# Feed-forward input units: one 512-column product for high and low activations, against two 256-column ones

## The chip, the cores and the metric

The program runs on one core of a Trainium2 chip. The metric is the device time of one execution in microseconds (us). Matrix products run on TensorE (PE; its weight loads are listed as PEld), element-wise work on VectorE (DVE), ScalarE (ACT) and GpSimd (POOL), and SyncE (SP) issues nearly all transfers.

## What is computed

Two transformer blocks of two layers each, in float32, on 256 tokens of width 1024. The first block has, in each layer, a gated feed-forward half, a mixer of three branches, a cross-attention and a second feed-forward half, each followed by a layer norm; the second block has adaptive modulation, attention over a latent and a context stream, and one feed-forward half per layer. The part that matters here is the gated feed-forward:

```python
def swiglu_ffn(x, w_in, w_out):          # x (256, 1024), w_in (1024, 5632), w_out (2816, 1024)
    a, b = jnp.split(x @ w_in, 2, axis=-1)
    return (jax.nn.silu(a) * b) @ w_out
```

It is computed six times: four times in the first block and once in the first layer of the second block for two streams, and once in the last layer for one stream.

## The kernel before

**Precision by splitting.** A float32 operand x is kept as a high part h (x rounded to fp32r by an ACT copy, line 200) and a low part l = x - h (a DVE subtraction, line 201). A product is then three matmuls into the same PSUM bank: high weights times high activations, high weights times low activations, low weights times high activations (`mm3`, lines 203 to 207). Each matmul instruction loads its own stationary 128x128 block of weights.

**Units.** `ffn_in` (from line 356) computes the 5632 columns of `x @ w_in` in 22 units of 2x128 columns: 128 for the gate a, 128 for the value b. The first two units go through `groupB` (activations stationary, then a transpose); the other 20, j = 2 to 21, keep the weights stationary and stream the 256 tokens. For one stream, `colsA` (line 209) makes 8 steps k of `mm3` for c = 0 (a) into columns 0 to 255 of one bank of the pool `pj`, then 8 for c = 1 (b) into columns 256 to 511: 48 matmuls of 256 columns. ACT then reads a through Silu (line 396), and DVE multiplies it with b (line 397). Five of the six passes are of this kind, 100 units in all; the pass over two streams has its own branch (lines 384 to 390), in which the two streams of 256 tokens stand side by side in a `Joint`, and matmuls have 512 columns.

**Weights.** `weight` (line 162) loads a unit as two halves of 512 KB (here c = 0 and c = 1), each into one of 3 buffers `wf`; ACT makes `wh` (6 buffers), DVE makes `wl` (5 buffers). The SP queue issues the loads in order. Between them stand the loads of `wa` (one buffer), rows of the modulation weights of the second block, which DVE multiplies with the condition vectors (line 913, two products for each load). These products have nothing to do with the feed-forward; `mods` (line 929) spreads them over the units of the first block.

**Order.** The instructions go through a scheduler, which orders each engine's queue by priority and by its own model of the engines; an engine then runs its queue strictly in that order. `issue_after` ties a few instructions behind others.

**Activations.** `Split` (line 41) holds h and l of all 8 steps in four tiles, each of 4 steps of one kind. It is written by `put`, in the tail of a layer norm (line 282) or of a modulation (line 958): for each of two token blocks, two groups of four transposes into PSUM, each followed by one split of 128x512.

**After the units.** `ffn_out` (line 400) multiplies with `w_out` in 11 units of 24 matmuls of 512 columns, into four banks of the pool `pa`. Both pools have four banks.

## Time and profile before

| | |
|---|---|
| median of 3 runs | 2544.79 us (2539.27, 2544.79, 2544.91) |
| the profiled execution | 2539.28 us, span of its records 2537.5 us |
| PE busy | 2441.2 us of the span |
| DVE, ACT, POOL busy | 1654.8, 1176.4, 67.2 us |
| mean granted TensorE clock | 0.984 of full speed |
| moved by DMA | 425.74 MB |

The profile lists busy times by engine and by group of instructions, the chain of work that ended last, and for every idle time of an engine what ended it. A matmul's record is longer than the step from one matmul to the next, since they are pipelined: the pace is read from the starts in the timeline. In each of the single-stream passes the 20 units run from about 22 to 137, 566 to 682, 765 to 881, 1302 to 1418 and 2356 to 2471 us; the pass over two streams from about 1781 to 1999 us.

### The profile page before, as it was taken

To read this page: it belongs to the slowest core of one execution; us is meant where nothing else is said; L and a number is where in the kernel's file an instruction comes from. 1 tells how busy PE (TensorE), PEld (TensorE's weight loads), DVE (VectorE), ACT (ScalarE), POOL (GpSimd) and SP (SyncE) were. 2 spreads that over 40 slices of the span, in tenths; PEclk is the share of its full clock that TensorE was granted. 3 is DMA by queue.
4 is the path that set the end of the run, shared out by engine and by line. 5 is a ranking of instruction groups with operands and counts; after the bars stand their busy time and mean duration, and the time that the engine had idled before them with its cause. 6 is when DMAs were issued, how large, how long until landed. Compare 5 with 4: busy or idle time off the path is not lost.

```text
span 2537.5 us, 39368 instructions
## 1 busy us (share of the span) xinstructions
PE 2441.2 (96%) x15166; PEld 2138.2 (84%) x15166; DVE 1654.8 (65%) x3277; ACT 1176.4 (46%) x1948; POOL 67.2 (3%) x88
## 2 busy tenths in 40 slices
PE   8999999989999999999899999899999999998999
PEld 8987999869979979999789877677888887776997
DVE  6576766578677667766677776776554537655554
ACT  5445564444444444555544545654222324545542
POOL 0000100000000000100000000000000000131000
PEclk9999999999999999999999999999999999998999
DMA  7774535547757755446557642013456633433564
GB/s 266 225 252 160 167 116 186 182 141 253 236 174 250 234 189 179 143 147 210 173 174 234 227 157 81 24 42 111 157 189 192 215 98 107 122 56 126 183 191 141
DMA packets 139420, 425.74 MB, mean 168 GB/s; under 512 B 29192, under 2 KB 36064, under 8 KB 139104
## 3 DMA queue, kind: packets, MB, share of 16 engines
q1 hardware_dynamic: 139232, 423.22, 52.3%
q8 instruction: 119, 1.95, 0.3%
q14 instruction: 69, 0.57, 0.1%
HBM read 417.89 MB, written 5.28 MB: 167 GB/s over the span
## 4 chain that ended last, share of the span: by engine, by line
PE 82%; DVE 9%; DMA 3%; ACT 3%; issue 1%; POOL 0%; SPq 0%; ACTq 0%; POOLq 0%; DVEq 0%
PE pj L205 18%; PE pj L206 18%; PE pj L207 18%; PE pa L206 7%; PE pa L205 7%; PE pa L207 7%; PE pa L278 3%; DVE wl L201 2%; DMA k<-in_rpbF_dram 1%; ACT wh L200 1%; DMA wf<-in_mix_A_dram 1%; DVE mx L463 1%; DVE rq L261 1%; DVE k L201 1%; DVE k L315 1%
## 5 line engine op out<-in xcount | busy, mean ns | idle before, releaser
L200 ACT CAST wh<-wf 128x1024 fp32r<-128x1024 f32 (+2 forms) x652 | 672.8, 1034 | 924.3 <-PE pj L206 240.9
L201 DVE TENSOR_TENSOR wl<-wf,wh 128x1024 fp32r<-128x1024 f32 (+2 forms) x652 | 782.3, 1204 | 443.4 <-PE pj L207 129.8
L205 PE MATMUL pj<-k,wh 128*128 128x256 f32 (+1 forms) x2896 | 840.7, 290 | 0.0
L206 PE MATMUL pj<-k,wh 128*128 128x256 f32 (+1 forms) x2896 | 837.9, 289 | 0.0
L207 PE MATMUL pj<-k,wl 128*128 128x256 f32 (+1 forms) x2896 | 837.2, 289 | 0.0
L205 PEld LDWEIGHTS pj<-k,wh 128*128 128x128 f32 x2896 | 554.4, 191 | 13.9 <-issue 6.4
L206 PEld LDWEIGHTS pj<-k,wh 128*128 128x128 f32 x2896 | 553.9, 191 | 9.3 <-issue 2.0
L207 PEld LDWEIGHTS pj<-k,wl 128*128 128x128 f32 x2896 | 553.9, 191 | 6.8
L206 PE MATMUL pa<-wl,k 128*128 128x512 f32 x688 | 273.8, 398 | 0.8 <-DVE wl L201 0.8
L205 PE MATMUL pa<-wh,k 128*128 128x512 f32 x688 | 272.1, 396 | 2.4 <-ACT k L200 2.4
L205 PE MATMUL pj<-wh,k 128*128 128x512 f32 (+1 forms) x616 | 252.3, 412 | 11.8 <-ACT wh L200 6.5
L206 PE MATMUL pj<-wl,k 128*128 128x512 f32 (+1 forms) x616 | 251.1, 408 | 3.1 <-DVE wl L201 3.0
L913 DVE SCALAR_TENSOR_TENSOR k<-wa,cond 128x1024 bf16<-128x1024 f32 x160 | 193.6, 1222 | 70.4 <-DMA wa<-in_mod_wT_dram 69.8
L207 PE MATMUL pa<-wh,a 128*128 128x512 f32 x560 | 217.6, 389 | 0.0
L207 PE MATMUL pj<-wh,k 128*128 128x512 f32 (+1 forms) x496 | 201.1, 407 | 1.1 <-DVE k L201 1.0
L205 PEld LDWEIGHTS pa<-wh,k 128*128 128x128 f32 x688 | 128.8, 187 | 36.6 <-ACT k L200 3.5
L205 PEld LDWEIGHTS pj<-wh,k 128*128 128x128 f32 x616 | 120.7, 196 | 40.2 <-ACT k L200 8.2
L206 PEld LDWEIGHTS pa<-wl,k 128*128 128x128 f32 x688 | 129.2, 188 | 28.8 <-DVE wl L201 1.1
L206 PEld LDWEIGHTS pj<-wl,k 128*128 128x128 f32 x616 | 120.8, 196 | 29.6 <-DVE wl L201 5.6
L278 PE MATMUL pa<-ident,k 128*128 128x128 f32 x516 | 86.8, 300 | 48.4 <-DVE k L315 21.0
L278 PEld LDWEIGHTS pa<-ident,k 128*128 128x128 f32 x516 | 63.8, 152 | 76.6 <-DVE k L315 27.5
L207 PEld LDWEIGHTS pa<-wh,a 128*128 128x128 f32 x560 | 105.3, 188 | 25.0
(253 smaller groups left out, 2418.3 us busy)
## 6 DMA issues: line engine op xcount, KB each, us to landing
wf<-in_ffn_w_inA_dram SPq DMA_DIRECT2D x262, 512.0 KB, 4.4
wf<-in_ffn_w_outB_dram SPq DMA_DIRECT2D x132, 512.0 KB, 4.4
wf<-in_mix_A_dram SPq DMA_DIRECT2D x108, 512.0 KB, 3.7
wa<-in_mod_wT_dram SPq DMA_DIRECT2D x96, 512.0 KB, 4.3
wf<-in_w_branchA_dram SPq DMA_DIRECT2D x32, 384.0 KB, 3.2
wf<-in_od_w_dram SPq DMA_DIRECT2D x24, 512.0 KB, 4.9
wf<-in_w_mix_outB_dram SPq DMA_DIRECT2D x16, 512.0 KB, 4.4
wf<-in_w_outB_dram SPq DMA_DIRECT2D x16, 512.0 KB, 4.1
```

What stands on the lines that cost most here:

```text
L200: self.nc.scalar.copy(h, x)
L201: self.nc.vector.tensor_tensor(l, x, h.bitcast(F32), ALU.subtract)
L205: mm(ps, sh, mh, start=start, stop=False)
L206: mm(ps, sh, ml, start=False, stop=False)
L207: self.mark = mm(ps, sl, mh, start=False, stop=stop).ins
L261: V.scalar_tensor_tensor(y2, a, 3 * s * s, y, ALU.subtract, ALU.mult)
L278: self.nc.tensor.transpose(ps[:, i * P:(i + 1) * P], b, self.ident)
L315: z = V.scalar_tensor_tensor(y[:, s], y[:, s], rs, gb[1][:, s], ALU.mult, ALU.add)
L463: V.reduce_max(mx[:, i:i + 1], ps[:, a:b], axis=AX.X, negate=scale == 1.0)
L913: V.scalar_tensor_tensor(junk, w, 1.0, self.cond[:, s], ALU.mult, ALU.mult, accum_out=mod[:, n, s:s + 1])
```

## The change

The activations of the single-stream passes are laid out in a new class `Sides`: a tile holds, for two steps k, the high parts and then the low parts, so that h and l of a step are read as one operand of 2x256 columns. A new `colsD` uses it: for each k, high weights times (h, l) in one 512-column matmul, which leaves high-by-high in the first half of a bank and high-by-low in the second; then low weights times h, 256 columns, added in the first half. A unit takes two banks, one of `pj` for a and one of `pa` for b. To read a bank out, ACT copies its second half to a buffer `k1`, and DVE adds the first half. Silu then reads the buffer on ACT, and the product of gate and value is made on POOL. Layer norms and modulations write `Sides`, with two splits of 128x256 in place of one of 128x512.

```diff
+class Sides:
+    def __init__(self, net):
+        self.hl = [net.k4(F32R).rearrange("p (s k t) -> p s k t", s=2, k=2) for _ in range(KT // 2)]
+    def h(self, k, c=slice(None)):
+        return self.hl[k // 2][:, 0, k % 2, c]
+    def l(self, k, c=slice(None)):
+        return self.hl[k // 2][:, 1, k % 2, c]
+    def both(self, k):
+        return self.hl[k // 2][:, :, k % 2]
+    def put(self, net, i, c, y):
+        for j in range(2):
+            t = self.hl[2 * i + j]
+            net.split(t[:, 0, :, c], t[:, 1, :, c], y[:, 2 * j:2 * j + 2])
...
+    def colsD(self, ps, w, base, xs):
+        mm = self.nc.tensor.matmul
+        for k in range(KT):
+            wh, wl = w.at(base + k * P, P)
+            mm(ps.rearrange("p (s t) -> p s t", s=2), wh, xs.both(k), start=k == 0, stop=False)
+            self.mark = mm(ps[:, :T], wl, xs.h(k), start=False, stop=k == KT - 1).ins
...
     def load_split(self, src):
-        xs = Split(self, KT)
+        xs = Sides(self)
...
-            self.split(xs.hs[i], xs.ls[i], f)
+            xs.put(self, i, slice(None), f)
...
     def post_ln(self, acc, x, scale, l, i, eps, want_xs=True):
-        xs = Split(self, KT) if want_xs else None
+        xs = Sides(self) if want_xs else None
...
-                ps = self.pj()
+                ab = []
                 for c in range(2):
-                    self.colsA(ps[:, c * T:(c + 1) * T], w, c * KT * P, P, streams[0])
-                a = self.k1()
-                nc.scalar.activation(a, ps[:, :T], AF.Silu)
-                nc.vector.tensor_tensor(gs[j // 4][:, j % 4], a, ps[:, T:], ALU.mult)
+                    ps = self.ps() if c else self.pj()
+                    self.colsD(ps, w, c * KT * P, streams[0])
+                    ab.append(self.k1())
+                    nc.scalar.copy(ab[c], ps[:, T:])
+                    nc.vector.tensor_tensor(ab[c], ab[c], ps[:, :T], ALU.add)
+                nc.scalar.activation(ab[0], ab[0], AF.Silu)
+                nc.gpsimd.tensor_tensor(gs[j // 4][:, j % 4], ab[0], ab[1], ALU.mult)
...
     def first_block(self, dbg=None, depth=DEPTH):
-        xs = Split(self, KT)
+        xs = Sides(self)
...
-                self.split(xs.hs[i][:, c], xs.ls[i][:, c], f[i][:, c])
+                for j in range(k // 2, (k + n) // 2):
+                    self.split(xs.hl[j][:, 0], xs.hl[j][:, 1], f[i][:, 2 * j % 4:2 * j % 4 + 2])
...
     def modulating(self, x, mod, kind, s, xs=None, aside=False):
-        xs = xs or Split(self, KT)
+        xs = xs or Sides(self)
```

## Rows read from the trace of the kernel before

**Rows 1.** The page: busy time by engine, and the chain's shares.

```profile
PE 2441.2 (96%) x15166; PEld 2138.2 (84%) x15166; DVE 1654.8 (65%) x3277; ACT 1176.4 (46%) x1948; POOL 67.2 (3%) x88
...
PE 82%; DVE 9%; DMA 3%; ACT 3%; issue 1%; POOL 0%; SPq 0%; ACTq 0%; POOLq 0%; DVEq 0%
```

**Rows 2.** Busy us, first pass: PE, PEld, DVE, ACT, POOL; clock, DMA share, GB/s.

```profile
22.00:137.50 115.50, 115.50 (x964) 115.41 (x962) 71.97 (x86) 51.51 (x65) 0.00 (x0) 1.00 0.75 237
```

**Rows 3.** Timeline of PE, last pass (start, duration, line): 256-column matmuls.

```profile
2400.11 0.28 PE L205 MATMUL pj<-k,wh 128*128 128x256 f32 x1
2400.23 0.28 PE L206 MATMUL pj<-k,wh 128*128 128x256 f32 x1
```

**Rows 4.** Five units of the last pass: DVE busy on low weights `wl`; clock, DMA.

```profile
2384.80:2413.60 28.80, 12.24 (x10) 1.00 0.60 185
```

**Rows 5.** DVE's group on low weights, last pass, 2362 to 2471 us.

```profile
L201 DVE TENSOR_TENSOR wl<-wf,wh 128x1024 fp32r<-128x1024 f32 x38 | 46.5, 1224 | 44.6 <-PE pj L207 34.2 <-issue 10.4
```

**Rows 6.** The same for three times five units of the third pass.

```profile
765.30:794.10 28.80, 11.01 (x9) 1.00 0.81 258
794.10:822.90 28.80, 10.82 (x9) 1.00 0.72 237
822.90:851.70 28.80, 13.16 (x11) 1.00 0.74 236
```

**Rows 7.** DVE's groups, third pass, 771 to 845 us: busy, mean ns, idle before.

```profile
L201 DVE TENSOR_TENSOR wl<-wf,wh 128x1024 fp32r<-128x1024 f32 x24 | 29.1, 1221 | 3.8 <-ACT wh L200 3.6
L913 DVE SCALAR_TENSOR_TENSOR k<-wa,cond 128x1024 bf16<-128x1024 f32 x21 | 25.1, 1222 | 6.2 <-DMA wa<-in_mod_wT_dram 6.1
L397 DVE TENSOR_TENSOR k<-k,pj 128x256 f32<-128x256 f32 x12 | 5.0, 419 | 3.9 <-ACT k L396 3.9
```

**Rows 8.** Timeline of PE, two-stream pass: first and last of six 512-column matmuls.

```profile
1799.95 0.39 PE L206 MATMUL pa<-k,wh 128*128 128x512 f32 x1
...
1801.08 0.39 PE L205 MATMUL pa<-k,wh 128*128 128x512 f32 x1
```

**Rows 9.** Timeline of PE: a 256-column matmul ahead of a 512-column one, and the reverse.

```profile
880.50 0.28 PE L207 MATMUL pj<-k,wl 128*128 128x256 f32 x1
880.62 0.40 PE L205 MATMUL pa<-wh,k 128*128 128x512 f32 x1
...
2355.80 0.39 PE L207 MATMUL pj<-wh,k 128*128 128x512 f32 x1
2356.03 0.28 PE L206 MATMUL pj<-k,wh 128*128 128x256 f32 x1
```

**Rows 10.** Timeline of PE, last `ffn_out`: its widest step between 512-column matmuls.

```profile
2489.81 0.40 PE L206 MATMUL pa<-wl,k 128*128 128x512 f32 x1
2490.05 0.39 PE L207 MATMUL pa<-wh,a 128*128 128x512 f32 x1
```

**Rows 11.** Line 396: count, min/median/max ns.

```profile
L396 ACT ACTIVATE k<-pj x100: 363/377/387, 28.3 to 2471.6; 128x256 f32<-128x256 f32 x100
```

**Rows 12.** Groups with shapes apart: a 256-column PSUM copy, splits of either size.

```profile
L376 ACT COPY k<-pa 128x256 f32<-128x256 f32 x14 | 5.2, 374 | 3.8 <-PE pa L278 3.8
...
L200 ACT CAST k<-pa 128x512 fp32r<-128x512 f32 x30 | 17.5, 585 | 20.8 <-PE pa L278 18.5 <-PE pa L819 1.5
...
L200 ACT CAST k<-pa 128x256 fp32r<-128x256 f32 x24 | 9.1, 393 | 1.1 <-PE pa L1396 1.1
...
L201 DVE TENSOR_TENSOR k<-pa,k 128x512 fp32r<-128x512 f32 x30 | 20.0, 688 | 8.6 <-ACT k L200 8.2
...
L201 DVE TENSOR_TENSOR k<-pa,k 128x256 fp32r<-128x256 f32 x24 | 9.9, 420 | 16.1 <-ACT k L200 15.9
```

**Rows 13.** Timeline of the mixer, second layer: POOL products beside a weight split.

```profile
1013.03 1.55 DVE L201 TENSOR_TENSOR wl<-wf,wh 128x1024 fp32r<-128x1024 f32 x1 [0.54 <-PE pj L207]
...
1012.77 0.73 POOL L657 TENSOR_TENSOR a<-k,sc 128x256 f32<-128x256 f32 x1
1013.46 1.44 POOL L658 TENSOR_TENSOR a<-k,sc 128x128 f32<-128x128 f32 x1
```

## Prediction

> **What bounds the kernel now.** I read the page first, then the stretches of the passes the change touches, then the queues that feed them. The page says that PE is busy for 96% of the span and carries 82% of the chain that ended last [rows 1]. By stretches it is plainer still: in the first pass PE is busy for all of 115.50 us at full granted clock, beside 71.97 us of DVE, 51.51 of ACT and none of POOL [rows 2]. PE's own pace is read from the starts: matmuls of 256 columns follow each other every 120 ns [rows 3], so a unit of 48 costs 5.76 us, and a half of its weights (24 matmuls) lasts 2.88 us. A pass of 20 units takes 115.2 us, nearly what the stretch shows: in the five single-stream passes nothing but PE sets the end today.
>
> Close behind PE is what feeds it: the load, the ACT cast and the DVE subtraction of each half of weights. Five units use ten halves, which are 12.24 us of DVE's subtraction [rows 4]. In the last pass exactly that is made, and DVE idles mainly until PE gives a buffer back [rows 5]: feeding is faster than eating, and the five `wl` buffers are full. The third pass differs. In its first two stretches DVE makes only 11.01 and 10.82 us of it, and catches up in the third with 13.16 [rows 6]. There the modulation products stand in DVE's queue; between 771 and 845 us, 21 of them take 25.1 us, and the idle of 6.2 us ahead of them ends when their own load lands [rows 7]. PE lives on the reserve for some nine units. The second and fourth passes show the same pattern in the same view; one stands for the three. In the first, `mods` is called only from j = 10 on. So the question is twofold: what PE saves, and whether the feeding follows.
>
> **PE's saving.** Per step k, three 256-column matmuls become one of 512 and one of 256; the columns stay the same. Three cost 3 x 120 = 360 ns. The 512-column form with the same read pattern (two runs of 256) exists in the pass over two streams, and steps there by 226 ns: 1.13 us for the five steps from the first to the last row of [rows 8]. Does the mixture add up? A 256-column matmul ahead of a 512-column one took 120 ns, a 512 ahead of a 256 took 230 as rounded [rows 9]. I expect 347 ns, 13 less. The 512-column steps of `ffn_out`, whose operands have other roles, are up to 240 ns wide [rows 10]; that would leave nothing. I take 227, what the rounding leaves at most, by the pass whose operands have the same roles and layout. For 16 steps and 100 units [rows 11] that is 16 x 100 x 0.013 = 20.8 us, or 4.16 us for each pass; a unit falls to 5.55 us, a half to 2.78.
>
> The Trainium skill, page "TensorE: Matmul & The Clock Gate", section "Back-to-back issue gap", gives a matmul a fixed part of 2.5 ns beside its columns at the warm clock. By that the change would save 2.5 ns per step, 4 us in all. The rows show 120 ns where 256 columns at 2.4 GHz are 106.7, so a fixed part near 13 ns, and I go by them.
>
> **Readout.** Removed per unit: a Silu from PSUM (0.377 us, ACT [rows 11]) and a product on DVE (0.419 [rows 7]). Added: two ACT copies of 256 columns (0.374 each [rows 12]), two DVE adds of the form of the old product (0.42 each), a Silu from SBUF (not in the trace; 0.36 to 0.39 by the PSUM form), and a POOL product. ACT gains 0.75 us a unit, DVE 0.42. ACT is busy for 51.51 of 115.50 us in the first pass [rows 2], so its part is hidden by idle time. The waits are new: the adds wait for ACT, and Silu on ACT for a DVE add, with the weight casts queued behind it; POOL waits for both, with nothing behind it. Banks: a unit takes one of four in each pool, as deep as the four single banks today, and `ffn_out` reaches the bank of the last unit only after 15 matmuls of at least 0.226 us, 3.4 us after its start; I cost that at nothing, up to 0.5 us a pass if the last add is late.
>
> **The POOL product** is the least certain. One of 128x256 takes 0.73 us undisturbed. But beside it a weight subtraction, which reads two SBUF tiles, took 1.55 us, and the POOL operation after it 1.44 [rows 13], against 1.221 for such a subtraction alone [rows 7]: POOL and DVE shut each other out. So a unit can cost DVE up to 0.42 + 0.73 = 1.15 us. How much delays the feeding? Nothing, where it falls into DVE's idle time; that is 6.2 + 3.8 + 3.9 = 13.9 us over 12 units [rows 7], 1.16 a unit, but part of it is the wait for ACT, which will not shrink. I take 0.5 us a unit, near the idle ahead of the modulation products (6.2 / 12), with 0 and 1.15 as ends.
>
> The Trainium skill, "GPSIMD Engine Reference", section "1. Specifications", says that POOL shares its SBUF interface with VectorE and that instructions with two SBUF inputs contend. This case's row agrees (1.55 us against 1.22), and by that rule the third rival below would hold.
>
> **Feeding, pass by pass.** In the first two stretches of the third pass (11.01 + 10.82) / 1.221 = 17.9 halves are made in 57.6 us, 6.44 us a unit for nine units. Against 5.55 us the reserve shrinks by 9 x 0.89 = 8.0 us. Full, it is four halves (the fifth buffer back comes free as its own half ends) less one subtraction and its hand-over, 4 x 2.78 - 1.3 = 9.8 us: 1.8 are left, and every further 0.1 us a unit takes 0.9. With 0.5 us PE waits 4.5 - 1.8 = 2.7 us, so such a pass keeps 4.16 - 2.7 = 1.5. At 0 it keeps all; at 1.15 it loses 4.4. Three passes give 4.4 us (ends: 12.5 gained, 13 lost). The last pass has no modulation products and its reserve is full: 4.16. The first has them in its second half alone, but starts with little reserve: 3.5 (1.5 to 4.2).
>
> **Splits.** A put now makes two casts of 0.393 in place of one of 0.585 and two subtractions of 0.420 in place of one of 0.688 [rows 12]: 0.20 us more on ACT, 0.15 on DVE. But the first of them ends earlier (0.393 + 0.420 = 0.81 against 1.27), and PE, waiting in the norm's tail, can start on two of four steps while the other pair is made. Some 13 norms and modulations stand on the path, each from 0.4 better to 0.3 worse: I take 0, with -5 and +4 us as ends. The scheduler also orders these tails anew; that lies within the same ends. No transfer is added or moved past another in the text of the kernel.
>
> **Sum.** 4.16 + 3.5 + 4.4 = 12 us off 2539.28 gives 2527 for an execution like the profiled one. That is the fastest of the three shown; the median lies 5.5 us higher, where the same share gives 2533. I name the middle, 2530.
>
> **Rivals.**
> - *All is hidden* (0.2). The product falls into idle time and the reserve suffices: 20.8 us, 2518. For it: 1.16 us of DVE idle a unit. Against: half of that follows ACT.
> - *No saving on PE* (0.07). The mixed stream steps by 240 + 120, or its fixed part is small: 0 to 4 us gained, 2535 to 2539, 2538 with feeding undisturbed. Against: [rows 8, 9].
> - *DVE and POOL become the bound* (0.23). Place: the nine units with modulation products in passes two to four. Price: 1.15 us a unit and a second wait for ACT, 0.3 (3.9 / 12): at 1.3 us PE waits 11.7 - 1.8 = 9.9, a loss of 5.7 a pass, 17 in three, against 4 won in the last, and none in the first: 2552. The total turns at 12.5 + 7.7 + 5.4 = 27 x, about 0.95 us a unit, and is slower by 0.3% from 1.23. In half of this rival's chance the price stays between these, about no change.
> - *The units do not run as the text has them* (0.05): a bank read late stops PE, for instance because ACT falls far behind; at 0.2 us a unit that eats the saving, 2539.
>
> **How the numbers follow.** The forecast has 0.45. A measurement here tells about 0.3% (7.6 us) from no change. Faster by more: the hidden case and most of the forecast, 0.2 + 0.38 = 0.58; slower by more: half of the third rival, 0.12; the rest, 0.30, lies within. The range runs from the hidden case with a little help by the splits, 2517, to the third rival's middle with the 5.5 us between the runs shown, 2546.
>
> **What would show it.** Starts of PE in a unit: 227 and 120 by turns (a first step above 235 refutes the saving). Gaps of PE in passes two to four around their sixth to fourteenth unit, none in the last pass, which should be 4.2 us shorter. Weight subtractions above 1.3 us beside POOL products. The idle time ahead of the modulation products shrinking from 6.2 us. The prediction fails if feeding slows by more than 1 us a unit, or not at all, or if a new order of the queues moves the norms' tails by more than 5 us.

## The result, and the profile after

The changed kernel takes 2562.94 us, median of 4 runs (2557.41 to 2565.94), beside 2544.61 for the kernel before on the same chip: a ratio of 1.0075 with an interval of 1.0052 to 1.0097. It is slower, by more than a measurement of this kernel needs to tell it from no change; the forecast was 2530, and 2562.94 lies outside its range.

From here on line numbers are the changed kernel's: 222 is the weight cast, 223 the subtraction, 227 to 229 the three matmuls of `mm3`, 244 and 245 the two of `colsD`, 428 the copy, 429 the addition, 430 Silu, 431 the product on POOL. The page after, beside [rows 1]: busy time, shares of the chain, and the group of PE's first matmul kind in `ffn_out` (busy us, mean ns, then idle before and what ended it):

```profile
PE 2433.8 (95%) x13566; PEld 2058.8 (81%) x13566; DVE 1707.3 (67%) x3430; ACT 1240.9 (49%) x2201; POOL 200.2 (8%) x188
...
PE 77%; DVE 9%; DMA 7%; ACT 4%; issue 2%; POOL 0%; SPq 0%; ACTq 0%; POOLq 0%; DVEq 0%
...
L227 PE MATMUL pa<-wh,k 128*128 128x512 f32 x688 | 276.5, 402 | 23.7 <-DVE k L429 16.2
```

PE's share of the chain fell from 82 to 77%, that of DMA rose from 3 to 7%, and PE now idles 23.7 us ahead of `ffn_out`'s matmuls: 16.2 of them until an addition of line 429 has ended, nearly all of the rest until a cast of `ffn_out`'s own activations has. The same group on the page of before:

```profile
L205 PE MATMUL pa<-wh,k 128*128 128x512 f32 x688 | 272.1, 396 | 2.4 <-ACT k L200 2.4
```

**The units themselves are faster, three passes of five by as much as forecast.** PE's timeline in the last pass (start, duration), beside [rows 3]:

```profile
2399.65 0.40 PE L244 MATMUL pj<-k,wh 128*128 128x512 f32 x1
2399.89 0.28 PE L245 MATMUL pj<-k,wl 128*128 128x256 f32 x1
2400.01 0.40 PE L244 MATMUL pj<-k,wh 128*128 128x512 f32 x1
...
2406.72 0.40 PE L244 MATMUL pj<-k,wh 128*128 128x512 f32 x1
```

And 20 steps k of the third pass, from the first row to the last:

```profile
800.07 0.39 PE L244 MATMUL pa<-k,wh 128*128 128x512 f32 x1
...
807.00 0.39 PE L244 MATMUL pa<-k,wh 128*128 128x512 f32 x1
```

Where three matmuls took 360 ns, the two take 347 in the third pass (20 steps in 6.93 us), and so in the first and the fourth. In the last pass they take 353 (20 steps, 2399.65 to 2406.72, in 7.07 us), and so in the second, over the whole pass, with the granted clock at 1.00 in both cases. So two passes of five get half of the saving. What decides it no run here shows; from kernel to kernel it falls on other passes, and on none in e15 below.

**The time is lost where the units hand over to `ffn_out`.** The end of the second pass in the profile after; first ACT, then DVE, then PE (in brackets the idle time ahead and what ended it):

```profile
689.33 1.05 ACT L222 CAST wh<-wf 128x1024 fp32r<-128x1024 f32 x1 [1.04 <-DMA wf<-in_ffn_w_outB_dram]
690.28 0.37 ACT L428 COPY k<-pj 128x256 f32<-128x256 f32 x1
691.14 0.42 ACT L430 ACTIVATE k<-k 128x256 f32<-128x256 f32 x1 [0.49 <-DVE k L429]
692.48 1.04 ACT L222 CAST wh<-wf 128x1024 fp32r<-128x1024 f32 x1 [0.92 <-DMA wf<-in_ffn_w_outB_dram]
693.43 0.37 ACT L428 COPY k<-pa 128x256 f32<-128x256 f32 x1
...
693.83 0.42 DVE L429 TENSOR_TENSOR k<-k,pa 128x256 f32<-128x256 f32 x1 [1.58 <-ACT k L428]
...
689.85 0.40 PE L229 MATMUL pa<-wh,a 128*128 128x512 f32 x1
694.30 0.79 PE L227 MATMUL pa<-wh,k 128*128 128x512 f32 x1 [4.05 <-DVE k L429]
694.89 0.63 PE L228 MATMUL pa<-wl,k 128*128 128x512 f32 x1
695.32 0.63 PE L229 MATMUL pa<-wh,a 128*128 128x512 f32 x1
```

The units ended at 686.59. PE makes 15 matmuls of `ffn_out` and then wants the `pa` bank of the last unit. It is read only at 693.83, because its copy on ACT stands behind a cast of `ffn_out`'s weights, and that cast waits for its transfer. The lateness as such is not new. In the profile before, ACT at the same place:

```profile
681.33 1.05 ACT L200 CAST wh<-wf 128x1024 fp32r<-128x1024 f32 x1 [2.49 <-DMA wf<-in_ffn_w_outB_dram]
682.28 0.38 ACT L396 ACTIVATE k<-pj 128x256 f32<-128x256 f32 x1
```

There a cast waited 2.49 us for a transfer too, with a unit's read-out behind it; but that read-out freed a bank of `pj`, which `ffn_out` of one stream doesn't use.

After the wait PE steps by 0.42 us instead of 0.23. The windows of the same place (busy us of PE, PEld, DVE, ACT, POOL; granted clock, DMA share, GB/s) show why:

```profile
692.40:699.20 6.80, 4.90 (x12) 3.84 (x13) 2.67 (x3) 2.98 (x4) 0.72 (x1) 0.50 0.75 271
699.20:754.50 55.30, 55.30 (x239) 44.46 (x237) 34.08 (x53) 23.03 (x27) 0.00 (x0) 1.00 0.55 183
```

For 6.8 us the granted clock is 0.5, the lower of the two levels. Such a stretch stands at the hand-over in four of the five passes. In the first of them PE waits longest for the cast of the activations, which stands behind the same late cast of weights in ACT's queue.

**Ledger.** From PE's starts in the timeline of each profiled execution: the time in units (five passes), from the last unit's end to the end of `ffn_out` (five), and the rest, in us. The last three columns are worked out against the row named. In passes two to four the traces of the new matmuls lack the first three records of the units, so their units column is some 1.4 us too low in all and the rest as much too high.

| kernel | units | to the end of `ffn_out` | rest | span | units | `ffn_out` | rest |
|---|---|---|---|---|---|---|---|
| before | 576.1 | 313.0 | 1648.4 | 2537.5 | | | |
| after (against before) | 557.9 | 343.2 | 1654.4 | 2555.5 | -18.2 | +30.2 | +6.0 |
| e8 (against before) | 558.1 | 328.7 | 1654.1 | 2540.8 | -18.0 | +15.7 | +5.7 |
| e12 (against before) | 565.7 | 324.3 | 1646.1 | 2536.1 | -10.4 | +11.3 | -2.3 |
| e11: before, 4 `wf` | 576.3 | 314.4 | 1641.4 | 2532.1 | | | |
| e10: after, 4 `wf` (against e11) | 556.7 | 322.7 | 1631.1 | 2510.4 | -19.6 | +8.3 | -10.3 |
| e16 (against e11) | 559.6 | 314.1 | 1632.8 | 2506.5 | -16.7 | -0.3 | -8.6 |
| e15 (against e11) | 553.9 | 313.3 | 1629.9 | 2497.1 | -22.4 | -1.1 | -11.5 |

### The profile page after: what moved, and what is told of

Its sections match the earlier page's. It is cut to its first block, busy times and chain, and to the rows that moved or that the text cites. A ratio compares the mean times of both kernels' runs of the same rounds, so it can differ in the third digit from the quotient of the medians.

```text
span 2555.5 us, 36748 instructions
## 1 busy us (share of the span) xinstructions
PE 2433.8 (95%) x13566; PEld 2058.8 (81%) x13566; DVE 1707.3 (67%) x3430; ACT 1240.9 (49%) x2201; POOL 200.2 (8%) x188
## 4 chain that ended last, share of the span: by engine, by line
PE 77%; DVE 9%; DMA 7%; ACT 4%; issue 2%; POOL 0%; SPq 0%; ACTq 0%; POOLq 0%; DVEq 0%
PE pj L227 10%; PE pj L228 10%; PE pj L229 9%; PE pj L244 7%; PE pa L227 7%; PE pa L228 7%; PE pa L244 7%; PE pa L229 7%; PE pj L245 4%; PE pa L245 3%; PE pa L309 3%; DVE wl L223 2%; DMA wf<-in_ffn_w_outB_dram 1%; DMA k<-in_rpbF_dram 1%; ACT wh L222 1%
## 5 line engine op out<-in xcount | busy, mean ns | idle before, releaser
L227 PE MATMUL pj<-k,wh 128*128 128x256 f32 (+2 forms) x1296 | 389.2, 300 | 0.0
L228 PE MATMUL pj<-k,wh 128*128 128x256 f32 (+2 forms) x1296 | 386.7, 298 | 0.0
L229 PE MATMUL pj<-k,wl 128*128 128x256 f32 (+2 forms) x1296 | 386.1, 298 | 0.0
L227 PE MATMUL pa<-wh,k 128*128 128x512 f32 x688 | 276.5, 402 | 23.7 <-DVE k L429 16.2
L244 PE MATMUL pj<-k,wh 128*128 128x512 f32 x800 | 284.4, 394 | 0.0
L244 PE MATMUL pa<-k,wh 128*128 128x512 f32 x800 | 284.0, 394 | 0.0
L227 PEld LDWEIGHTS pj<-k,wh 128*128 128x128 f32 (+1 forms) x1296 | 248.5, 192 | 13.5 <-issue 6.4
L228 PEld LDWEIGHTS pj<-k,wh 128*128 128x128 f32 (+1 forms) x1296 | 248.6, 192 | 9.0 <-issue 2.0
L229 PEld LDWEIGHTS pj<-k,wl 128*128 128x128 f32 (+1 forms) x1296 | 248.8, 192 | 6.7
L245 PE MATMUL pj<-k,wl 128*128 128x256 f32 x800 | 224.6, 281 | 0.0
L245 PE MATMUL pa<-k,wl 128*128 128x256 f32 x800 | 224.3, 280 | 0.0
L431 POOL TENSOR_TENSOR k<-k,k 128x256 f32<-128x256 f32 x100 | 133.1, 1331 | 1090.5 <-DVE k L429 1053.8
L227 PEld LDWEIGHTS pa<-wh,k 128*128 128x128 f32 x688 | 131.1, 191 | 60.8 <-DVE k L429 18.2
L244 PEld LDWEIGHTS pj<-k,wh 128*128 128x128 f32 x800 | 150.2, 188 | 34.6
```

What stands on the lines that cost most here:

```text
L227: mm(ps, sh, mh, start=start, stop=False)
L228: mm(ps, sh, ml, start=False, stop=False)
L229: self.mark = mm(ps, sl, mh, start=False, stop=stop).ins
L244: mm(ps.rearrange("p (s t) -> p s t", s=2), wh, xs.both(k), start=k == 0, stop=False)
L245: self.mark = mm(ps[:, :T], wl, xs.h(k), start=False, stop=k == KT - 1).ins
L431: nc.gpsimd.tensor_tensor(gs[j // 4][:, j % 4], ab[0], ab[1], ALU.mult)
```

## The experiments

Theory H: the last units' banks are read late, behind casts that wait for transfers, and `ffn_out` waits for them. The rivals to it: F, the feeding with DVE and POOL in each other's way is the loss; N, the new layout with its splits costs the time; and that the matmuls' saving itself isn't worth what the starts say.

### Which part: the layout, the second bank, the pool that the awaited bank comes from

**e3_layout**: the layout `Sides` and its splits, with the units and their read-out as before.

```diff
...
-                    self.colsD(ps, w, c * KT * P, streams[0])
...
+                    self.colsA(ps[:, c * T:(c + 1) * T], w, c * KT * P, P, streams[0])
...
```

> The new layout of the activations alone: Sides in place of Split, with two splits for one, and the units as before (three matmuls of 256 columns, one bank, Silu and a DVE product). Rival N (tails): the 6 to 7 us that the changed kernel loses between a pass's ffn_out and the next pass appear here: 2550 (2547 to 2554). Theory H: nothing lost, 2539 to 2546, no PE wait after a pass.

Measured: 2543.94 us, ratio 0.9996 (0.9984 to 1.0008). Layout and splits cost nothing, as the term of 0 had it; N falls.

**e4_bank**: the kernel before, with b in a bank of its own from `pa`.

```diff
-                ps = self.pj()
+                ab = []
                 for c in range(2):
-                    self.colsA(ps[:, c * T:(c + 1) * T], w, c * KT * P, P, streams[0])
+                    ab.append(self.ps() if c else self.pj())
+                    self.colsA(ab[c][:, :T], w, c * KT * P, P, streams[0])
...
```

> The kernel before with one part of the change: a unit's b in a bank of its own from pa, products, layout and read-out as before (Silu on ACT, product on DVE). Theory H, as the trace of before has it: the last read-out ends some 1.5 us behind the pass, ffn_out needs that bank after 2.8 us at the earliest, so no wait, 2539 to 2548: the late bank needs the late read-out too. If the bank alone is enough, PE waits of 3 us or more stand after passes one to four, and the time is 2555 to 2565.

Measured: 2547.66 us, ratio 1.0007 (0.9995 to 1.0020). A `pa` bank at the hand-over is not enough by itself, with the old matmuls and the old read-out. The times of e3 and e4 stand clear of the changed kernel's; those of the next two runs do not.

**e1_swap**: a in `pa`, b in `pj`, so that the bank `ffn_out` waits for is read half a unit earlier.

```diff
-                    ps = self.ps() if c else self.pj()
+                    ps = self.pj() if c else self.ps()
```

> The changed kernel with the two banks of a unit exchanged: the gate a goes to the pool pa, the value b to pj. The pa bank that is read last is then that of the last unit's a, one cast and one copy earlier in ACT's queue. Theory H (hand-over: ffn_out takes the four pa banks over from the units and waits for the last read-out of one): PE's waits after passes one to four, 6.2, 4.5, 7.6 and 5.7 us in the changed kernel, shrink by 2 to 4 us each, and the median falls from 2563 to about 2548 (2543 to 2556). Rival F (the feeding of weights, slowed by DVE's and POOL's new work, sets the time): no change, 2557 to 2566. Rival N (the split tails of the norms): no change either.

Measured: 2556.26 us, ratio 1.0055 (1.0033 to 1.0077). From start to start, PE's gaps at the hand-over shrink to 3.5 to 3.8 us in the first three passes (from 6.7, 4.5 and 6.3). The median is 7 us below that of the changed kernel, but the two intervals overlap, and the profiled execution is the fastest of its four: H in part, by the gaps alone.

**e2_pj**: both banks from `pj`.

```diff
-                    ps = self.ps() if c else self.pj()
+                    ps = self.pj()
```

> The changed kernel with both banks of a unit taken from pj, so that pa is free when ffn_out starts. Theory H: the waits after passes one to four go, and with them the half clock behind them, some 27 to 30 us: 2535 (2530 to 2543), if PE does not wait inside a pass for pj, which is then two units deep (11.1 us) against read-outs that lag by up to 8 us. Rival F: 2557 to 2566, the waits move into the passes. Rival N: as F, with no waits in the passes.

Measured: 2555.91 us, ratio 1.0047 (1.0030 to 1.0064). In the second and third pass the waits for a bank at the hand-over are gone (61.5 us to the end of `ffn_out`, as before), but with `pj` only two units deep PE now waits inside the passes. All its waits for line 429 (us in total, times, longest):

```profile
PE pj L244 <- DVE k L429: 12.7, 14, 2.2
```

So the read-out is late all along the pass; with two pools nobody waits for it until the pass ends. The time is far from the 2535 us that H promised, and its interval overlaps that of the changed kernel: the wait has moved.

### Why it is late: POOL, ACT's queue, or the transfers

**e5_dve**: the product on DVE.

```diff
-                nc.gpsimd.tensor_tensor(gs[j // 4][:, j % 4], ab[0], ab[1], ALU.mult)
+                nc.vector.tensor_tensor(gs[j // 4][:, j % 4], ab[0], ab[1], ALU.mult)
```

> The changed kernel with one edit: the product of a unit runs on VectorE again, not on GpSimd. Late-bank theory (the last unit's bank is read late because its copy stands behind weight casts in ScalarE's queue, and ffn_out, which takes the same four banks, waits for it): the copy is no earlier, so the gaps of 4.5 to 6.7 us at the hand-over and the half-clock stretches behind them stay, and the time is 2555 to 2566 us, as the changed kernel's 2563. Rival, GpSimd in VectorE's way (subtractions beside the product are up to 1.75 us long): the gaps shrink with the shorter subtractions and the time falls to 2545 us or less. Rival, VectorE becomes the bound: 32 units of 0.42 us more in five passes, and gaps appear inside the passes; 2566 us or more.

Measured: 2562.79 us, ratio 1.0078 (1.0048 to 1.0108), and PE's wait for line 429 is no shorter (in the slowest of the four executions, which is the profiled one):

```profile
L227 PE MATMUL pa<-wh,k 128*128 128x512 f32 x688 | 277.6, 403 | 28.7 <-DVE k L429 21.3 <-ACT k L222 7.4
...
L223 DVE TENSOR_TENSOR wl<-wf,wh 128x1024 fp32r<-128x1024 f32 x35 | 42.6, 1221 | 0.6 <-ACT wh L222 0.6
```

In the second pass (the second row, 580 to 685 us) a subtraction takes 1.221 us again, as in the kernel before, and ACT's weight casts still wait 41.8 us for transfers, as in the changed kernel (40.4). POOL is not the cause, and DVE doesn't become the bound by the product: F falls in both its forms.

**e6_queue**: a unit's weight casts behind the copy of the second bank three units earlier.

```diff
+        read = self.reads.pop(0) if self.reads else None
...
-                with self.after(self.holds[0]):
+                with self.after(self.holds[0]), self.after(read):
...
+        if n == 1:
+            self.reads = [None] * 3
...
-                    nc.scalar.copy(ab[c], ps[:, T:])
+                    read = nc.scalar.copy(ab[c], ps[:, T:]).ins
...
+                self.reads.append(read)
```

> The changed kernel with ScalarE's queue put in another order: the weight casts of a unit stand behind the copy of the second bank three units earlier, so that the last copies stand ahead of most of ffn_out's casts. Nothing else is changed. Late-bank theory: the gaps at the hand-over fall from 4.5 to 6.7 us to about before's (2 us in the first pass, none in the others), no half-clock stretch of 6.8 us follows, ffn_out's part of a pass is 61.5 us again, and with the 18 us that the units save the time is 2526 to 2540 us, faster than before. If the casts that now wait for copies starve TensorE instead, the gaps come back inside the passes and the time is 2545 to 2560. Rival, the gaps come from something other than the order of the queue (GpSimd, DMA at ffn_out's weights): they stay at 4 us or more and the time stays near 2560.

Measured: 2554.60 us, ratio 1.0052 (1.0033 to 1.0071): 8 us below the changed kernel, where H promised 23 or more, and with overlapping intervals. ACT (this kernel's lines stand two to five further down: 224 is the cast, 432 the copy) at the end of the first pass, where PE's gap is 6.3 us long and ends at 139.37:

```profile
135.57 0.35 ACT L432 COPY k<-pa 128x256 f32<-128x256 f32 x1
137.38 1.04 ACT L224 CAST wh<-wf 128x1024 fp32r<-128x1024 f32 x1 [1.46 <-DMA wf<-in_ffn_w_outB_dram]
138.33 0.46 ACT L528 COPY k<-pa 8x384 f32<-8x384 f32 x1
138.70 0.61 ACT L224 CAST k<-k 128x512 fp32r<-128x512 f32 x1
```

Here the copy does come before the late cast. But behind the same cast stands the cast of `ffn_out`'s first activations (138.70), and PE needs that as well. The wait only changes its name: what is late is whatever follows the late transfer in ACT's queue. In the second and the third pass the edit missed its aim: there PE's gaps are 5.0 and 4.1 us and still end with the addition, and in the second the last copy stands again behind a cast that waits 2.14 us for its transfer. (The profiled execution is the slowest of the seven.)

**e7_last**: b in `pj` in the last four units, so that no bank of `ffn_out` is read late.

```diff
-                    ps = self.ps() if c else self.pj()
+                    ps = self.ps() if c and j < FT - 4 else self.pj()
```

> The changed kernel with the second bank of a pass's last four units taken from the other four banks, so that the banks that ffn_out takes were all read several units before; ScalarE's queue is as it was. Late-bank theory: the gaps at the hand-over go although the copies are as late as before, short waits for banks may appear in the last four units (those banks are then two units deep, 7 us), and the time is 2528 to 2545 us. Rival, ffn_out waits for its weights or for GpSimd: gaps of 4 us or more stay at its first steps, time near 2560.

Measured: 2550.90 us, ratio 1.0035 (1.0021 to 1.0049). It is faster than the changed kernel, though short of the 2545 us that H allowed at most. The second and third `ffn_out` take 61.5 us again, at the price of gaps of 2.5 and 2.9 us in the last units; in the first pass a gap of 7.1 us stays, for the reason that e6 shows (the profiled execution is the slowest of the ten):

```profile
137.52 1.04 ACT L222 CAST wh<-wf 128x1024 fp32r<-128x1024 f32 x1 [1.71 <-DMA wf<-in_ffn_w_outB_dram]
138.47 0.36 ACT L428 COPY k<-pj 128x256 f32<-128x256 f32 x1
138.74 0.46 ACT L523 COPY k<-pa 8x384 f32<-8x384 f32 x1
139.11 1.13 ACT L222 CAST k<-k 128x512 fp32r<-128x512 f32 x2
```

**e8_noadd**: the new matmuls without the added read-out; the second half of each bank, high weights times low activations, is left out of the result.

```diff
...
-                    nc.scalar.copy(ab[c], ps[:, T:])
-                    nc.vector.tensor_tensor(ab[c], ab[c], ps[:, :T], ALU.add)
-                nc.scalar.activation(ab[0], ab[0], AF.Silu)
-                nc.gpsimd.tensor_tensor(gs[j // 4][:, j % 4], ab[0], ab[1], ALU.mult)
+                nc.scalar.activation(a, ab[0][:, :T], AF.Silu)
+                nc.vector.tensor_tensor(gs[j // 4][:, j % 4], a, ab[1][:, :T], ALU.mult)
```

> The changed matmuls alone: the 512-column product is issued as in the change, but its second half is left out of the read-out (the product of the high weights and the low activations is so left out of the result); Silu and the product read the first halves straight from the two banks, as the kernel before reads its bank. So it has TensorE's saving without the two copies, the two additions and the product on GpSimd. If a step of 512 and 256 columns saves 13 ns and nothing else of the matmuls costs time: 20.8 us less in the sum, at most 2 us a pass given back at the hand-over, 2523 to 2536 us. If the time stays at 2545 or more, the matmuls' own form takes the gain back and the late-bank theory is at best half of it.

Measured: 2542.49 us, ratio 0.9994 (0.9978 to 1.0011). This was the surprise. The added read-out explains 20 us of the changed kernel (2562.9 to 2542.5), and yet nothing is left of the matmuls' saving without it: the units save 18.0 us, and 15.7 go again before the end of `ffn_out` (6.9 in the third pass, 7.9 in the fourth) and 5.7 elsewhere. In the third pass it is a bank once more. Line 429, here the product of gate and value, frees it, and its Silu stands behind a cast that waits for a transfer:

```profile
872.03 1.04 ACT L222 CAST wh<-wf 128x1024 fp32r<-128x1024 f32 x1 [2.14 <-DMA wf<-in_ffn_w_outB_dram]
...
875.13 0.79 PE L227 MATMUL pa<-wh,k 128*128 128x512 f32 x1 [3.77 <-DVE k L429]
```

In the fourth pass five gaps of 0.8 to 3.2 us add up, behind DVE and ACT. So the longer read-out is at best half of the cause; a bank that is read behind late casts stays without it.

**e12_tail4**: the last four units as before (three matmuls, one bank of `pj`).

```diff
+            elif j >= FT - 4:
+                ps = self.pj()
+                for c in range(2):
+                    self.colsA(ps[:, c * T:(c + 1) * T], w, c * KT * P, P, streams[0])
...
```

(Of the 20 units that the change touches, 16 keep the new form here and 18 in e16; the expectations count 18 and 20 of 22, with the first two, which never had it.)

> The changed kernel with the last four units of each single-stream pass in the form of before (three 256-column products a step, both halves in one bank of the other four, Silu and the product straight from it): 18 units of 22 keep the saving, and at the hand-over neither late copies nor banks of ffn_out's are in the way. Late-bank theory: ffn_out's part is 61.5 us in the second and third pass and 63.5 in the first, the units save 15 us, the stretches between lose some 4 us as in all runs with the new units, and the time is 2528 to 2540 us, faster than before. Rival, TensorE simply arrives earlier than the weights whatever reads the banks: gaps of 3 us or more at ffn_out's first steps in two or more passes, 2542 us or more.

Measured: 2537.08 us, ratio 0.9976 (0.9956 to 0.9995), the first that is faster than before, if only just. `ffn_out` is about as long as before in the second and third pass; 6.0 us are lost in the first and 4.9 in the fourth, with nothing waiting for a read-out. First the group in `ffn_out`, then PE's longest wait in the fourth pass, in this run and in the profile before:

```profile
L227 PE MATMUL pa<-wh,k 128*128 128x512 f32 x688 | 274.2, 399 | 6.2 <-ACT k L222 5.9 <-ACT wh L222 0.3
...
1450.11 0.69 PE L309 MATMUL pj<-ident,k 128*128 128x128 f32 x2 [2.80 <-DVE k L1014]
...
1450.81 0.41 PE L278 MATMUL pj<-ident,k 128*128 128x128 f32 x2 [1.40 <-DVE k L972]
```

In the first pass what remains is the cast of activations behind the late transfer. In the fourth it is not: there PE's transposes for the second block, which stand inside `ffn_out`, wait 1.4 us longer for DVE, and 6.8 us at the lower clock go with it. With the read-out out of the way, the question became the transfers.

### The transfers: a fourth landing buffer

Four runs with `wf` at 4 buffers; to make room, `k4` has 19 for 20.

```diff
-            wf = self.t([P, UNIT // 2], "wf", 3, pool=self.wp)[:, :half]
+            wf = self.t([P, UNIT // 2], "wf", 4, pool=self.wp)[:, :half]
...
-        return self.t([P, 1024], "k4", 20, dt)
+        return self.t([P, 1024], "k4", 19, dt)
```

**e10_wf4**, the changed kernel with them:

> The changed kernel with a fourth landing buffer for weights (wf) and, to make room, one k4 buffer fewer (19 for 20). Late-bank theory in its sharper form (the last read-out stands in ScalarE's queue behind a cast that waits for a late transfer of ffn_out's weights, so the lateness of the transfer is passed on to TensorE): with transfers a buffer earlier the casts no longer wait 2 to 3 us for them, the hand-over gaps fall from 4.5 to 6.7 us to 2 us or less and the time to 2525 to 2545 us. Rival, the read-out is late because of the number of instructions in the queue and not of the transfers: gaps and time stay as in the changed kernel, 2555 to 2565 us. Fewer k4 buffers can cost something elsewhere, which the kernel before with the same two edits, run beside it, tells.

**e11_before_wf4**, the kernel before with them:

> The kernel before with the same two edits (four landing buffers, 19 k4 buffers), for comparison with the changed kernel under them. If transfers bind neither its units nor its ffn_out, as its reserve of 8 to 10 us at the end of each pass says, it stays at 2538 to 2548 us; if the fourth buffer shortens the stretches between the passes, it falls below 2538.

**e13_tail4_wf4**, e12 with them:

> The last four units in the form of before and the fourth landing buffer together. If both the late read-out and the late transfers count, it is the fastest of the four, 2520 to 2535 us; if the fourth buffer does nothing or its room costs as much, it is as the run with the four units alone.

Measured: e10 2513.26 us, ratio 0.9877 (0.9862 to 0.9891); e11 2534.91, 0.9960 (0.9945 to 0.9975); e13 2511.04, 0.9866 (0.9849 to 0.9883). e10 and e13 are faster than either expectation had them. Under four buffers the change is a gain of 21.7 us (2534.9 to 2513.3); under three a loss of 18.3. ACT's group of weight casts in the second pass shows what the buffer does; after (580 to 685 us), then e10 (560 to 663):

```profile
L222 ACT CAST wh<-wf 128x1024 fp32r<-128x1024 f32 x36 | 37.8, 1050 | 42.1 <-DMA wf<-in_ffn_w_inA_dram 37.7 <-DMA wf<-in_ffn_w_outB_dram 2.7 <-PE pa L244 1.5
```

```profile
L222 ACT CAST wh<-wf 128x1024 fp32r<-128x1024 f32 x36 | 37.6, 1046 | 16.8 <-DMA wf<-in_ffn_w_inA_dram 14.0 <-PE pj L244 1.6 <-DMA wf<-in_ffn_w_outB_dram 0.6
```

36 casts waited for 40.4 us for transfers, 1.1 us each; now for 14.6. Read-outs stood behind these waits in ACT's queue. At the end of the first pass in e10 the last casts wait for no transfer, and the last copy is made at 131.46, 1.2 us after the last unit's last matmul began (130.26); after, it was made at 137.45:

```profile
129.54 0.42 ACT L430 ACTIVATE k<-k 128x256 f32<-128x256 f32 x1 [0.49 <-DVE k L429]
130.51 1.04 ACT L222 CAST wh<-wf 128x1024 fp32r<-128x1024 f32 x1 [0.55 <-PE pa L244]
131.46 0.36 ACT L428 COPY k<-pa 128x256 f32<-128x256 f32 x1
```

PE's waits ahead of this kind of matmul in `ffn_out` fall from 23.7 to 7.8 us:

```profile
L227 PE MATMUL pa<-wh,k 128*128 128x512 f32 x688 | 273.7, 398 | 7.8 <-DVE k L429 4.9 <-ACT k L222 2.8
```

The buffer does not quicken the feeding as a whole. Averaged over the records of the second pass, casts follow each other every 2.89 us in the kernel after and in e10, where PE eats a half in 2.83 and in 2.78: in both the reserve shrinks through that pass. What changes is where the lateness lies. ACT's copies are no longer late, but ACT now waits for DVE's additions ahead of its Silu, 31.0 us in the same window of e10 beside 6.3 in the kernel after:

```profile
L430 ACT ACTIVATE k<-k 128x256 f32<-128x256 f32 x17 | 7.1, 419 | 31.0 <-DVE k L429 31.0
```

At the hand-over this leaves PE the 4.9 us for line 429 above.

**e14_k19**, the changed kernel with the smaller `k4` alone:

> The changed kernel with 19 k4 buffers for 20 and nothing else. If the gain of the run with four landing buffers is that of the landing buffer, this one is as the changed kernel or slower, 2555 to 2575 us. If fewer k4 buffers change the order or the room of other transfers for the better, it is below 2550.

Measured: 2565.78 us, ratio 1.0088 (1.0061 to 1.0114). The gain comes with the landing buffer. Its room and the order that the scheduler makes of it are not told apart: by starts in the traces, some 145 of ACT's 2201 instructions and 94 of the 880 transfers stand at another place in e10 than in the kernel after (6 and 5 in e14).

**e15_noadd_wf4**, e8 with four buffers:

> The changed matmuls without the added read-out (the product of the high weights and the low activations is left out of the result), with four landing buffers and 19 k4 buffers. If the read-out costs time only where transfers are late, it is within 6 us of the run with the read-out and four landing buffers: 2505 to 2514 us. If the read-out costs TensorE something by itself, it is lower, 2500 or less. If the matmuls' saving of 20.8 us is all there is to be had, it is not far from 2534.9 less 20.8, 2514 us.

**e16_tail2_wf4**, four buffers and the last two units as before:

> Four landing buffers, 19 k4 buffers, and only the last two units of a pass in the form of before, so that 20 units of 22 keep the saving. If the 2.5 and 3.2 us that remain at the hand-over of the second and third pass come from the banks of the last units: ffn_out's part is 61.5 us there, and the time is 2505 to 2513 us. If the last two units are too few, for the copies of the unit before them still stand behind late casts: 2511 to 2516 us.

Measured: e15 2503.56 us, ratio 0.9848 (0.9830 to 0.9865), between its two expectations; e16 2508.59, 0.9869 (0.9850 to 0.9887). PE's group in `ffn_out` for e15 and for e16:

```profile
L227 PE MATMUL pa<-wh,k 128*128 128x512 f32 x688 | 272.1, 396 | 2.5 <-ACT k L222 2.5
```

```profile
L227 PE MATMUL pa<-wh,k 128*128 128x512 f32 x688 | 272.9, 397 | 2.8 <-ACT k L222 2.8
```

Both have before's 2.4 us again, give or take 0.4. So with transfers earlier the read-out still costs 9.7 us by the medians (e10 less e15; 7.4 by their ratios, since they ran on two chips). In the profiled executions it is 13.3, of which 9.4 stand in the `ffn_out` column of the ledger; 2.1 more are one pass in which e10 has the longer step of 353 ns and e15 has not. Giving the last two units their old form takes that column back to e11's, for 2.9 us in the units. Together:

| median us | 3 `wf` buffers | 4 `wf` buffers |
|---|---|---|
| kernel before | 2544.6 | 2534.9 |
| new matmuls, no added read-out | 2542.5 | 2503.6 |
| the change | 2562.9 | 2513.3 |
| the change, last units as before | 2537.1 (four units) | 2511.0 (four), 2508.6 (two) |

Neither cause makes the loss alone. With three buffers the new matmuls gain 2 us, which is not told from nothing, and the read-out costs 20; with four they gain 31 (28.5 by the ratios), and the read-out costs 10. e16 and e13 beat both kernels, by 1.3%; between them and e10 the intervals overlap.

What stays open: of the gain under four buffers, 10.3 us (e10 against e11) and 11.5 (e15 against e11) lie in none of the places that the change touches, in the column of the rest. The stretch between the fourth and the fifth pass, 867 us for 874, holds most of it, and the clock may be much of that. In e11 PE is at the lower level for 10.2 us at one place, in e10 for 3.4 and then back at the upper (the 10.2 us of e11, then the 6.8 that follow the 3.4 in e10; columns as above):

```profile
1647.37:1657.60 10.23, 9.69 (x38) 7.44 (x40) 6.24 (x19) 4.73 (x12) 0.00 (x0) 0.50 0.00 0
...
1640.30:1647.10 6.80, 6.54 (x48) 5.04 (x46) 5.92 (x18) 3.91 (x10) 0.00 (x0) 0.99 0.00 0
```

Summed over the stretch, the granted clock is at 0.50 for 47.8 us in e11 and for 34.1 in e10 and in e15. At 427 ns a step for 231 that is up to 6 of the 7 us, an estimate. No run shows whether the change brings this about or the accident of where the waits fall. In the kernel after, the rest is 6.0 us longer than before though this stretch is 2.4 shorter; that was not followed.

## Why the prediction was wrong, step by step

**PE's saving: right in three passes, half of it in two.** 347 ns a step were forecast and are seen in the first, third and fourth pass; the first takes 111.1 us for 115.3. In the second and the last the step is 353, so that the last pass is 2.0 us shorter and not 4.2, and its 512-column matmuls step by 237 ns on average, above the 235 that were to refute the saving. It is halved there, not gone. The five passes' units save 18.2 us in the profiled execution, some 17 with the missing records, of 20.8 by the sum, which took one step for all passes. By the fixed part of 2.5 ns that the Trainium skill gives ("TensorE: Matmul & The Clock Gate", section "Back-to-back issue gap"), 4 us would have come; the trace bears out the 13 ns read from the rows in three passes and 7 in two, and the rival "no saving on PE" falls.

**Feeding inside the passes: too dark.** I took 2.7 us of waits in each of the passes two to four. There were none, and the page has no idle time at all ahead of the two kinds of matmul in the units. The size of the disturbance was over-rated; in the second pass, besides, PE's longer step asked for less. DVE's and POOL's groups in the second pass, 580 to 685 us:

```profile
L223 DVE TENSOR_TENSOR wl<-wf,wh 128x1024 fp32r<-128x1024 f32 x36 | 48.0, 1338 | 1.1 <-ACT wh L222 0.9
L948 DVE SCALAR_TENSOR_TENSOR k<-wa,cond 128x1024 bf16<-128x1024 f32 x20 | 25.6, 1288 | 5.5 <-DMA wa<-in_mod_wT_dram 5.5
...
L431 POOL TENSOR_TENSOR k<-k,k 128x256 f32<-128x256 f32 x18 | 25.2, 1402 | 324.8 <-DVE k L429 309.9 <-issue 6.4 <-PE pj L245 5.5
```

A subtraction is 0.117 us longer than the 1.221 of [rows 7], a modulation product 0.066, and a unit has two subtractions and about one product: 0.3 us of contention a unit, which is gone in e5 (1.221 us for both). The product on POOL takes 1.40 us here instead of the 0.73 of [rows 13]. What the Trainium skill says ("GPSIMD Engine Reference", section "1. Specifications"), that the two engines contend, holds in this trace. But the rival built on it doesn't: moved back to DVE, the product changes the time by nothing (e5).

**Read-out and banks: the step that failed.** I wrote that `ffn_out` reaches the last unit's bank 3.4 us after its start, and costed the hand-over at nothing, up to 0.5 us a pass if the last addition is late: the wait at the hand-over is the term that failed. The first half is right: PE stops 3.3 us after the last unit (686.59 to 689.85). The other half needed the end of that addition, and I never worked it out. I counted ACT's time by its busy share, [rows 2], and called it hidden; but the read-out is not hidden by idle time when the idle time is a wait in the same queue ahead of it. In the profile before ACT idled 46.1 us for transfers of this kind in the second pass, and that row stood one view away from the one I read for DVE:

```profile
L200 ACT CAST wh<-wf 128x1024 fp32r<-128x1024 f32 x38 | 39.9, 1051 | 59.5 <-DMA wf<-in_ffn_w_inA_dram 46.1 <-DVE wl L201 4.7 <-DVE k L913 4.0
```

Three changes meet at this point: a read-out with one more hop (ACT's copy, then DVE's addition), a bank that `ffn_out` needs at once, and a PE that arrives with a smaller reserve, so that the casts of `ffn_out`'s first halves wait for transfers just then. The cost was 30.2 us in the profiled execution: 21.3 of waits (23.7 less 2.4), and 9 more. The four stretches at the lower clock hold about 44 matmuls, each 0.196 us longer than at the upper, which makes 8.6, an estimate. Of the waits, 16.2 us are the read-out's, in passes two to four; the first pass's is that of the cast of activations, for which the prediction had no term at all.

**The reserve was priced at the wrong place.** I asked how far it falls while PE is inside a pass and let it end there. A reserve that lasts just to the end of the pass is spent in the first halves of `ffn_out`. e8 shows it, in which the read-out has before's form and the saving is gone all the same, and e10 against e11 shows the reverse: the casts' waits for transfers fall, and the saving stays.

**Splits: right** (e3: 0 of 7.6 us that can be told).

**The rivals.** "All is hidden" was right on the units' waits, which did not come. "The units do not run as the text has them" had the mechanism, a bank read late that stops PE, but at a price of 0.2 us a unit spread over the pass, and with a chance of 0.05. It came as 6 to 9 us in one place of four passes. The chance of slower, 0.12, belonged wholly to a rival that didn't come.

## What to carry to other kernels

An engine's idle time hides added work only if the work does not stand behind the wait that makes the idle time: look at what ends the idle time in the queue that gets the new instruction, and at which buffer that instruction frees. A faster bound engine can spend its suppliers' reserve and pay at the next stage that shares the buffers, not where it became faster, as here. So a saving on the bound engine and one more landing buffer are to be tried together: here the one alone cost 18 us, the other alone gave 10, and both gave 31, some 10 of them at places that the change does not touch.

## What the runs showed of the hardware

- At the hand-over, where PE is idle for 4.1 to 5.9 us at a time, its granted clock falls to 0.5 within the wait and is there for 6.8 us each time (692.4 to 699.2 in the rows above, in a wait that ends at 694.30). Matmuls of 512 columns then step by 427 ns instead of 231. Some 9 to 13 of them fall into each stretch, 1.8 to 2.5 us more: the wait's price is the wait and that. The stretches of the first, third and fourth pass:

```profile
136.00:142.80 6.80, 4.05 (x10) 3.19 (x11) 3.30 (x5) 2.72 (x5) 1.65 (x1) 0.50 0.62 232
893.80:900.60 6.80, 3.82 (x9) 3.05 (x10) 1.65 (x2) 2.36 (x3) 0.73 (x1) 0.50 0.69 251
1439.90:1446.70 6.80, 5.52 (x13) 4.37 (x14) 4.78 (x20) 4.46 (x8) 0.73 (x1) 0.50 0.23 73
```

- Matmuls of 512 and 256 columns by turns step by the sum of their own steps (0.227 and 0.120 us) in three of five passes of the kernel after, 347 ns, with no bubble between, though the second adds into half of the bank that the first fills. In the other two passes the pair takes 353, all through the pass, at the same granted clock. What makes the difference is not shown.
